# The second FFN of layer 0 in chunks of 4, 4, 4, 4 and 6, with its last down products begun from a doubled x in PSUM

## The chip, the core and the metric

The kernel is one program on one core of a Trainium2 chip. The core has five engines that run side by side, each with its own instruction queue: TensorE (PE in the profile; its weight loads are PEld), VectorE (DVE), ScalarE (ACT), GpSimd (POOL) and SyncE (SP). DMA queues bring data from memory into the on-chip buffer. TensorE writes its results into PSUM banks, from where VectorE and ScalarE read them. Engines wait for each other through semaphores. The metric is the device time of one execution, in microseconds; the median of three executions of the kernel before is 2505.7 us.

## The reference, cut to what matters

Two layers run over T = 640 tokens (512 of a prompt and 8 x 16 of running streams) of width D = 1024. Each has a half-step FFN, a mixer (a short convolution and banded attention, gated) and a second half-step FFN. All is fp32.

```
x = x + 0.5 * swiglu1(rmsnorm(x))
x = x + mixer(rmsnorm(x))
x = x + 0.5 * swiglu2(rmsnorm(x))

def swiglu(h):                       # FF = 2816
    g, u = split(h @ w_gu)           # 1024 x 5632
    return (silu(g) * u) @ w_down    # 2816 x 1024
```

The four FFNs are called a0, b0 (layer 0, before and after the mixer), a1 and b1 (layer 1). The change concerns b0, and the start of a1, which follows b0 directly.

## The kernel before

**Layout and products.** x is held transposed, as eight tiles `x[0]` to `x[7]` of 128 features by 640 tokens. An fp32 operand is split into a high part (a cast to the fp32r type) and a low part (what the cast left), and a product is made of three fp32r matmuls: high with high, low with high, high with low. Each covers 320 tokens, a half of the tokens (`HT`), and a 128 x 128 tile of weights. Weight slabs are fetched by DMA (`source`, L271), ScalarE casts their high part `whi` (L321) and VectorE subtracts for the low part `wlo` (L326).

**Seven products instead of eight.** The large products are made by a scheme that treats the operands as 2 x 2 blocks (the two halves of the tokens are one of the two block directions) and needs seven block products for eight, at the price of sums on VectorE. Their operands are called X11, X21, XN6, XT5, XT7, X22 and XT4. For x this is done in `Expand.final(m)` (L539): for each `x[m]` ScalarE squares it for the norm (L610), scales it (L559) and casts it, and VectorE makes sums and the low parts (L561 to L591). At odd m the sums need the even tile before, so the last cast (L576) waits for VectorE (L571). `Expand.weights(m)` (L594) takes care of the next slabs.

**An FFN.** The 22 feature tiles of FF are cut into chunks; `FFNS` (L46) lists the sizes of the chunks and how many tiles at the start go without the scheme. For each tile j, `gate_up` (L773) makes its gate and its up product in 84 matmuls (`paa`, `pba`, `pca` and so on in the profile), and a tail that ends in the activation, cast into `ahi` (L228) and its low part; the tail is put into the queues at a later place, and the last tile's after its last matmul. When a chunk is done, its down product is added to x during the next chunk. There are two ways:

- A chunk of exactly 4 tiles that isn't the last goes by seven (`by_seven`, L81). Two tiles make a `Pair` (L905), whose casts are ahead in `Pair.product`, and `down_rows` (L966) makes four outputs at a time, twice, behind gate-ups 1 and 2 of the next chunk: 84 matmuls each (L982), with results that ScalarE stages (L996, L999), GpSimd adds to x by accumulating DMAs (L1004), or VectorE takes straight from PSUM (L1009).
- Other chunks go plain: for each output m, `product` runs 6 matmuls per tile of the chunk (L388) into one PSUM accumulator, and VectorE does `x = 0.5 * pd + x` (L1119).

The last chunk is always plain, because nothing of this FFN follows to cover it: its eight products stand at the end, and as each `x[m]` comes out, `nxt.final(m)` prepares it for the next FFN. In b0 before, the chunks are 2, 4, 4, 4 and 8.

**Order and buffers.** The order of TensorE's, VectorE's and ScalarE's queues is that of the program text in most places. `flush` and `prep` in that text decide where a weight cast and its low part stand. From gate-up `free` (L1060) to the "cut" ahead of the last products only TensorE's order is fixed, and a scheduler sets the others. The accumulators of the plain products and of the rows come from a pool (`acc`) of two buffers of two banks each. The first gate-up of an FFN (`first` in `gate_up`) has an order of its own, in which the norm's sums of the new x are made as well.

Of the kernel before, what the change touches and what calls it, by code (L numbers as in the profile page):

```python
# [16 lines left out]
P = 128  # L17
# [25 lines left out]
NT = T // P  # L43


FFNS = {"a0": ((4, 4, 4, 4, 4, 2), 4), "b0": ((2, 4, 4, 4, 8), 0),  # L46
        "a1": ((4, 4, 4, 4, 4, 2), 0), "b1": ((3, 4, 4, 4, 4, 3), 0)}

PARTS = slice(0, 3 * P), slice(3 * P, T)
# [135 lines left out]
def halves(t):  # L185
    return t.rearrange("p (a b) -> p a b", a=2)
# [3 lines left out]
def trunk(ctx: ExitStack, tc: tile.TileContext, xin, wst, small, pbias, samplebias, kcache, vcache,  # L190
# [190 lines left out]
    def soon():  # L381
        return tc.high_priority(offset=300)

    def multiply(ps, ws, xs, first, last):
        (wh, wl), (xh, xl) = ws, xs
        for j, (w, x) in enumerate(((wh, xh), (wh, xl), (wl, xh))):
            for a in range(2):
                PE.matmul(ps[:, a, :HT], w, x[:, a * HT : (a + 1) * HT],  # L388
                          start=first and j == 0, stop=last and j == 2)

    def steps(ps, ops, at=()):


        n = len(ops)
        for k, (xh, xl) in enumerate(ops):
            if k in at:
                at[k]()
            multiply(ps, tiles.take(), (xh, xl), k == 0, k == n - 1)
            yield

    def product(ps, ops, at=()):
        for _ in steps(ps, ops, at):
            pass

    def block(ps, s, half, ops, ks, start, stop):
# [12 lines left out]
        ACT.dma_start(sm[:, c], small[:, c])  # L418
    ident = cp.tile([P, P], F32, name="ident")
    make_identity(nc, ident)  # L420
    ones = cp.tile([P, P], F32, name="ones")
    POOL.memset(ones, 1.0)
    fold = cp.tile([P, HP], F32, name="fold")
    POOL.tensor_tensor(out=fold, in0=ident[:, :HP], in1=ident[:, HP:], op=ALU.add)
# [48 lines left out]
    class Stats:  # L473
# [34 lines left out]
        @staticmethod  # L508
        def rows(ps, turned):

            for i in range(2):
                q = slice(i * HP, (i + 1) * HP)
                PE.matmul(ps[i], ones[q], turned[q, : ps[i].shape[1]], start=True, stop=True)

        def spread(self, ps, turned, out):

# [9 lines left out]
    class Expand(Stats):  # L526
# [67 lines left out]
        def weights(self, m):  # L594


            if m == KT - 3:
                source(used[0] + 3)
            elif m == KT - 1:
                self.flush()  # L600
                ahead()
                flush()
                begin()
# [126 lines left out]
    def seven(n, bank, X, c1, u2, c5, first, second, third, last):  # L730
# [39 lines left out]
        with soon():  # L770
            last(pa)

    def gate_up(fp, n, ex, first, tails, put, j, pair, later, at):  # L773

        pa, pb, pc = (att(f"p{i}{n}")[:, :HT] for i in "abc")

        def cap(name):
            return fp.tile([P, 2, HT], F32, tag="cap", name=f"{name}{n}", bufs=5)

        def mul(ps, s, half, x, ks, start, stop):  # L780
            block(ps, s, half, lambda kp: tuple(z[:, x] for z in ex.ops[kp]), ks, start, stop)

        def spot(name):
            step(later, f"g{at}{name}")

        every, most, end = range(NP), range(NP - 1), range(NP - 1, NP)
        g, u = tmp(f"g{n}"), tmp(f"u{n}")
        t1, t2 = slice(0, HT), slice(HT, T)
        both = cap("c1_")
        c1, u2, c5 = both[:, 0], both[:, 1], cap("c5_")[:, 0]  # L790
        rho = ex.rho
        if first:

            new = not ex.known
            s0, s1 = quiet(), quiet()
            mul(pa, s0, 0, X11, every, True, True)
            ACT.copy(c1, pa)
            if ex.rest:
                ex.rest()
            flush()  # L800
            if new:
                add(ex.ssum, ex.ssum, ex.sq6)
                ex.add()
            for t in tails[:2]:
                t()
            mul(pc, s1, 1, XT5, every, True, True)
            ACT.copy(c5, pc)
            if new:
                mul(pb, s0, 1, X21, most, True, True)
                mul(pa, s1, 0, XN6, most, False, True)  # L810
                mul(pb, s0, 1, X21, end, True, True)
                mul(pa, s1, 0, XN6, end, False, True)
            else:
                mul(pa, s1, 0, XN6, every, False, True)
                mul(pb, s0, 1, X21, every, True, True)
            ACT.copy(u2, pa)
            add(u[:, t1], pb, c1)
            for t in tails[2:]:
                t()
            tails.clear()  # L820
            s2 = quiet()
            prep(len(ready))
            flush()

            def third():
                mul(pc, s2, 1, X22, every, False, True)
                add(u[:, t2], pc, u2)

            if new:
                third()  # L830
                ex.total(acc(f"nps{n}")[:, 0])
                ex.root()
                ex.diagonal()
                prep(len(ready))
            mul(pa, s2, 0, XT7, every, False, True)
            add(g[:, t2], pa, c5)
            flush()
            if new:
                nbc = acc(f"nbc{n}")
                ex.spread([nbc[:, a, :HT] for a in range(2)])  # L840
            DVE.tensor_tensor(out=g[:, t2], in0=g[:, t2], in1=rho[:, t2], op=ALU.mult)
            if not new:
                third()
                prep(len(ready))
                flush()
            s3 = slab(True)[0]
        else:
            s0 = quiet()
            mul(pa, s0, 0, X11, every, True, True)
            ACT.copy(c1, pa)  # L850
            prep(used[0] + 1)
            spot("e1")
            for t in tails:
                t()
            tails.clear()
            spot("e2")
            flush()
            mul(pb, s0, 1, X21, every, True, True)
            add(u[:, t1], pb, c1)
            s1 = slab(True)[0]  # L860
            flush()
            mul(pa, s1, 0, XN6, every, False, True)
            ACT.copy(u2, pa)  # L863
            spot("e3")
            mul(pc, s1, 1, XT5, every, True, True)
            ACT.copy(c5, pc)
            s2 = slab(True)[0]
            spot("e4")
            mul(pa, s2, 0, XT7, every, False, True)
            add(g[:, t2], pa, c5)  # L870
            DVE.tensor_tensor(out=g[:, t2], in0=g[:, t2], in1=rho[:, t2], op=ALU.mult)
            flush()
            ahead()
            mul(pc, s2, 1, X22, every, False, True)
            add(u[:, t2], pc, u2)
            s3 = slab(True)[0]
            ahead()
        mul(pa, s3, 0, XT4, every, False, True)
        DVE.tensor_tensor(out=g[:, t1], in0=pa, in1=rho[:, t1], op=ALU.mult)
        ACT.activation(g, g, AF.Silu, scale=-1.0)  # L880
        spot("e7")
        flush()

        def tail(weights=True):
            if weights:
                begin()
            DVE.tensor_tensor(out=g, in0=g, in1=rho, op=ALU.mult)
            hi = hp.tile([P, T], F32R, tag="hhi", name=f"ahi{n}")
            lo = hp.tile([P, T], F32R, tag="hlo", name=f"alo{n}")
            if pair:  # L890
                pair.product(n, u, g, hi, lo)
            else:
                DVE.tensor_tensor(out=u, in0=u, in1=g, op=ALU.mult)
                flush()
                split(hi, lo, u)
            put(j, (hi, lo))
            if weights:
                ahead()

        tails.append(tail)  # L900

    class Pair:
# [5 lines left out]
            self.fp, self.name, self.i, self.later, self.spots = fp, name, i, later, spots  # L908
            self.E, self.X, self.done = None, {}, 0

        def product(self, n, u, g, hi, lo):
            if self.E is None:

                z = self.E = self.fp.tile([P, 3, HT], F32, name=f"de{n}", tag="even", bufs=1)
                DVE.tensor_tensor(out=z[:, 0:3:2], in0=halves(u), in1=halves(g), op=ALU.mult)
                DVE.tensor_tensor(out=z[:, 1], in0=z[:, 0], in1=z[:, 2], op=ALU.subtract)
                at, kinds = slice(0, 2), (X11, XT5)
            else:

                z = self.O = self.fp.tile([P, 5, HT], F32, name=f"do{n}", tag="odd", bufs=1)  # L920
                DVE.tensor_tensor(out=z[:, 3:5], in0=halves(u), in1=halves(g), op=ALU.mult)
                at, kinds = slice(3, 5), (X21, X22)
                self.later.append(self)
                self.work = self.rest()
            flush()
            ACT.copy(halves(hi), z[:, at])
            self.low(halves(lo), halves(hi), z[:, at])
            self.keep(kinds, hi, lo)

        def low(self, lo, hi, z):  # L930
            DVE.tensor_tensor(out=lo, in0=z, in1=hi.bitcast(F32), op=ALU.subtract)
# [117 lines left out]
    def ffn(name, fp, ex, goff, after, end=False):  # L1049
# [6 lines left out]
        last = FT - chunks[-1]  # L1056
        hold[0] = True

        mode = ExitStack()
        free = min(j for j in range(FT) if by_seven(name, j)) + 2  # L1060

# [7 lines left out]
        for what, a in ffn_order(name):  # L1069
# [29 lines left out]
            if end and js[0] == last:  # L1099
                nxt.all([act[j] for j in js])  # L1100
                break
            for m, js in a:
                if js[0] == last and m < 2 and first_two:

# [814 lines left out]
```

## Time and profile before

| | |
|---|---|
| runs | 2505.62, 2505.7 and 2506.22 us; median 2505.7 |
| profiled execution | 2506.73 us, of which the instruction span is 2505.0 us |
| mean granted TensorE clock | 0.998 of full speed |
| TensorE busy | 2487.9 us (99%), 17472 matmuls |
| VectorE busy | 2123.9 us (85%), 3443 instructions |
| ScalarE busy | 1322.0 us (53%), 2069 instructions |
| GpSimd busy | 254.2 us (10%), 378 instructions |

A row of the profile gives the start, the duration, the engine, the line of the program, the operation and its output and input tiles with shapes; `x12` says that twelve instructions alike are merged. Square brackets hold the idle time of that engine just ahead, and the engine, tile and line that ended it. The number and the letter behind a name (`pdb`, `paa`) are an FFN (a or b) and a part; numbers of tiles are left out. A row of grouped instructions has the count, then the busy time in us and the mean in ns, then the idle time ahead of them. A windows row gives for a stretch of the span the busy time of each engine with the number of its instructions, the granted clock, the share of the DMA engines and their GB/s. In this execution b0 runs from about 839 to 1257 us, and a1 follows it up to about 1670 us.

### The profile page before, as it was taken

The page shows a single profiled execution, that of the slowest core. Times are in us where ns is not written, and L with a number is a line of the kernel's source. Part 1 is how long each engine was busy: PE and PEld are TensorE (multiplying, and loading weights), DVE is VectorE, ACT ScalarE, POOL GpSimd, SP SyncE. Part 2 cuts the span into 40 slices and gives each one's busy share as a digit, 9 for nine tenths or more (in the row PEclk, how much of TensorE's full clock was granted, in tenths as well). Part 3 has the DMA queues.
Part 4 walks back from the last instruction along what each step waited for, and adds up shares of the span by engine and source line. Part 5 has one row for each costly group of instructions (what it writes and reads, how often), then busy time and mean ns, then how long its engine had stood idle before and what let it go on. Part 6 is the DMA issues. An engine that isn't in the chain of part 4 may idle for free.

```text
span 2505.0 us, 43861 instructions
## 1 busy us (share of the span) xinstructions
PE 2487.9 (99%) x17472; PEld 2433.1 (97%) x17472; DVE 2123.9 (85%) x3443; ACT 1322.0 (53%) x2069; POOL 254.2 (10%) x378
## 2 busy tenths in 40 slices
PE   9999999999999999999999999999999999999998
PEld 8999999889999999999999999998899999999998
DVE  7889998888677899998699999988786768899997
ACT  7445556664444545555455555556644455455553
POOL 0001112112000001110001111121210000011111
PEclk9999999999999999999999999999999999999999
DMA  4233445334222234443224343443432222244434
GB/s 145 76 102 103 121 116 127 108 122 156 77 87 92 76 102 116 108 108 101 85 75 110 110 121 103 116 118 118 140 136 85 77 93 78 86 113 109 121 101 103
DMA packets 101005, 265.47 MB, mean 106 GB/s; under 512 B 11360, under 2 KB 46816, under 8 KB 100800
## 3 DMA queue, kind: packets, MB, share of 16 engines
q1 hardware_dynamic: 69408, 220.76, 27.3%
q0 software_dynamic: 30528, 41.26, 9.3%
q8 instruction: 137, 2.24, 0.4%
q10 hardware_dynamic: 864, 0.65, 0.1%
q14 instruction: 68, 0.56, 0.1%
HBM read 222.70 MB, written 7.94 MB: 92 GB/s over the span
## 4 chain that ended last, share of the span: by engine, by line
PE 96%; DVE 2%; ACT 1%; DMA 1%; issue 0%; SPq 0%; DVEq 0%; ACTq 0%
PE pab L411 12%; PE paa L411 11%; PE pcb L411 6%; PE pca L411 6%; PE daa L982 5%; PE py L388 4%; PE po L388 4%; PE qa L411 4%; PE dab L982 4%; PE pdb L388 4%; PE pbb L411 3%; PE pba L411 3%; PE dca L982 3%; PE ma_cv L411 2%; PE ma_qk L411 2%; PE pda L388 2%
## 5 line engine op out<-in xcount | busy, mean ns | idle before, releaser
L321 ACT CAST whi<-raw 128x1024 fp32r<-128x1024 f32 (+1 forms) x566 | 509.5, 903 | 391.7 <-PE pbb L411 38.6
L326 DVE TENSOR_TENSOR wlo<-raw,whi 128x1024 fp32r<-128x1024 f32 (+1 forms) x566 | 585.4, 1037 | 137.7 <-ACT whi L321 135.5
L321 ACT CAST whi<-s 128x1024 fp32r<-128x1024 f32 (+1 forms) x152 | 144.4, 950 | 261.0 <-issue 89.5
L411 PE MATMUL pab<-xhib,whi 128*128 128x320 f32 x704 | 218.1, 310 | 0.0
L411 PE MATMUL pab<-xhib,wlo 128*128 128x320 f32 x704 | 217.3, 309 | 0.0
L411 PE MATMUL pab<-xlob,whi 128*128 128x320 f32 x704 | 217.3, 309 | 0.0
L411 PE MATMUL paa<-xhia,whi 128*128 128x320 f32 x640 | 198.1, 309 | 0.8 <-ACT c_a L863 0.5
L411 PE MATMUL paa<-xloa,whi 128*128 128x320 f32 x640 | 197.6, 309 | 0.0
L411 PE MATMUL paa<-xhia,wlo 128*128 128x320 f32 x640 | 197.6, 309 | 0.0
L326 DVE TENSOR_TENSOR wlo<-s,whi 128x1024 fp32r<-128x1024 f32 (+1 forms) x152 | 166.0, 1092 | 3.4 <-ACT whi L321 3.4
L1004 POOL DMA_DIRECT2D x<-c_b x56 | 49.2, 1017 | 1066.6 <-DVE x L1009 782.5
L1004 POOL DMA_DIRECT2D x<-c_a x72 | 63.4, 1017 | 831.6 <-ACT whi L321 508.0
L411 PEld LDWEIGHTS pab<-xhib,whi 128*128 128x128 f32 x704 | 132.1, 188 | 1.4 <-issue 0.9
L411 PEld LDWEIGHTS pab<-xlob,whi 128*128 128x128 f32 x704 | 132.1, 188 | 0.0
L411 PEld LDWEIGHTS pab<-xhib,wlo 128*128 128x128 f32 x704 | 132.1, 188 | 0.0
L411 PEld LDWEIGHTS paa<-xhia,whi 128*128 128x128 f32 x640 | 120.2, 188 | 1.8 <-ACT c_a L863 0.7
L411 PEld LDWEIGHTS paa<-xloa,whi 128*128 128x128 f32 x640 | 120.2, 188 | 0.0
L411 PEld LDWEIGHTS paa<-xhia,wlo 128*128 128x128 f32 x640 | 120.2, 188 | 0.0
L411 PE MATMUL pcb<-xhib,wlo 128*128 128x320 f32 x352 | 108.9, 309 | 0.0
L411 PE MATMUL pcb<-xhib,whi 128*128 128x320 f32 x352 | 108.7, 309 | 0.0
L411 PE MATMUL pcb<-xlob,whi 128*128 128x320 f32 x352 | 108.6, 309 | 0.0
L265 DVE TENSOR_TENSOR raw<-raw,raw 128x512 f32<-128x512 f32 x152 | 103.8, 683 | 1.8 <-DMA raw<-in_wst 1.3
(680 smaller groups left out, 7971.2 us busy)
## 6 DMA issues: line engine op xcount, KB each, us to landing
raw<-in_wst SPq DMA_DIRECT2D x378, 512.0 KB, 3.6
x<-c_a POOLq DMA_DIRECT2D x72, 160.0 KB, 4.2
x<-c_b POOLq DMA_DIRECT2D x56, 160.0 KB, 3.8
kc<-in_kcache SPq DMA_DIRECT2D x32, 256.0 KB, 3.7
vc<-in_vcache SPq DMA_DIRECT2D x16, 512.0 KB, 4.6
x<-u_a POOLq DMA_DIRECT2D x36, 160.0 KB, 4.2
x<-u_b POOLq DMA_DIRECT2D x28, 160.0 KB, 4.1
bias<-in_pbias POOLq DMA_DIRECT2D x16, 256.0 KB, 3.7
```

The costliest lines, as they stand in the source:

```text
L265: DVE.tensor_tensor(out=out, in0=a, in1=b, op=ALU.add)
L321: ACT.copy(hi[:, d], src[:, c])
L326: DVE.tensor_tensor(out=lo, in0=src, in1=hi.bitcast(F32), op=ALU.subtract)
L388: PE.matmul(ps[:, a, :HT], w, x[:, a * HT : (a + 1) * HT], start=first and j == 0, stop=last and j == 2)
L411: PE.matmul(ps, a, b, start=start and kp == 0 and j == 0, stop=stop and kp == NP - 1 and j == 2, skip_group_check=True)
L982: PE.matmul(ps[u], w, y, start=start and i == 0 and j == 0, stop=i == 1 and j == 2, skip_group_check=True)
L1004: POOL.dma_start(x[ms[2 * u + r]][:, cols], z[:, u], accum_op=ALU.add)
```

## The change

The chunks of b0 become 4, 4, 4, 4 and 6. One chunk more goes by seven, and the plain last chunk has 6 tiles instead of 8. Beside this:

- The eight last products of b0 no longer start from zero. ScalarE writes 2 x `x[m]` into the PSUM accumulator (`seed`), all matmuls accumulate onto it, and ScalarE, not VectorE, writes back `x[m]` as half of the result. Seeds 0 and 1 come ahead of product 0; seed m+1 stands in the program between the evacuation of `x[m-1]` with its `final`, and product m. Only b0 takes this way (`nxt` and a last chunk longer than 4).
- The first gate-up's pair casts its high part and subtracts its low part later: `held` keeps them until the `u2` copy of the next gate-up (a0's first pair, b0's and a1's).
- The column of ones for the norm's sums is one column wide and broadcast where it is used as a matrix.
- `weights` finds its next slab by a search instead of a fixed distance.

```
-FFNS = {"a0": ((4, 4, 4, 4, 4, 2), 4), "b0": ((2, 4, 4, 4, 8), 0),
+FFNS = {"a0": ((4, 4, 4, 4, 4, 2), 4), "b0": ((4, 4, 4, 4, 6), 0),
...
+    def seed(ps, m, scale):
+        ACT.activation(two(ps), halves(x[m]), AF.Copy, scale=scale)
...
-    def multiply(ps, ws, xs, first, last):
+    def multiply(ps, ws, xs, first, last, seeded=False):
...
-                          start=first and j == 0, stop=last and j == 2)
+                          start=first and j == 0 and not seeded, stop=last and j == 2,
+                          skip_group_check=seeded)
...
-    ones = cp.tile([P, P], F32, name="ones")
+    ones = cp.tile([P, 1], F32, name="ones")
...
-                PE.matmul(ps[i], ones[q], turned[q, : ps[i].shape[1]], start=True, stop=True)
+                PE.matmul(ps[i], ones[q].to_broadcast([HP, P]), turned[q, : ps[i].shape[1]], start=True, stop=True)
...
-                source(used[0] + 3)
+                source(next(i for i in range(used[0], len(slabs)) if slabs[i][0] == "gu" and slabs[i][2] == 1))
...
             ACT.copy(u2, pa)
+            for t in held:
+                t()
+            held.clear()
             spot("e3")
...
-                pair.product(n, u, g, hi, lo)
+                pair.product(n, u, g, hi, lo, held if first else None)
...
+            def parts():
+                ACT.copy(halves(hi), z[:, at])
+                self.low(halves(lo), halves(hi), z[:, at])
             self.keep(kinds, hi, lo)
+            if held is None:
+                parts()
+            else:
+                held.append(parts)
...
+        def seeded_down(name, a, js, nxt):
+            def begun(m):
+                pds[m] = acc(f"pd{name}_{js[0]}_{m}")
+                seed(pds[m], m, 2.0)
+            for m, _ in a:
+                if m == 0:
+                    begun(0)
+                if m + 1 < KT:
+                    begun(m + 1)
+                pd = pds.pop(m)
+                product(pd, [act[j] for j in js], seeded=True)
+                nxt.weights(m)
+                ACT.activation(halves(x[m]), two(pd), AF.Copy, scale=0.5)
+                if m < KT - 1:
+                    flush()
+                nxt.final(m)
...
+            if nxt and len(js) > 4:
+                seeded_down(name, a, js, nxt)
+                continue
```

More of the change, by code (lines that the diff above doesn't have):

```diff
@@ L388, in multiply, with steps @@
                 PE.matmul(ps[:, a, :HT], w, x[:, a * HT : (a + 1) * HT],
-                          start=first and j == 0, stop=last and j == 2)
-    def steps(ps, ops, at=()):
+                          start=first and j == 0 and not seeded, stop=last and j == 2,
+                          skip_group_check=seeded)
+    def steps(ps, ops, at=(), seeded=False):
         n = len(ops)
@@ L397, in steps, with product @@
                 at[k]()
-            multiply(ps, tiles.take(), (xh, xl), k == 0, k == n - 1)
+            multiply(ps, tiles.take(), (xh, xl), k == 0, k == n - 1, seeded)
             yield
-    def product(ps, ops, at=()):
-        for _ in steps(ps, ops, at):
+    def product(ps, ops, at=(), seeded=False):
+        for _ in steps(ps, ops, at, seeded):
             pass
@@ L771, in seven @@
             last(pa)
+    held = []
     def gate_up(fp, n, ex, first, tails, put, j, pair, later, at):
@@ L909, in __init__, with product @@
             self.E, self.X, self.done = None, {}, 0
-        def product(self, n, u, g, hi, lo):
+        def product(self, n, u, g, hi, lo, held=None):
             if self.E is None:
@@ L925, in product @@
             flush()
-            ACT.copy(halves(hi), z[:, at])
-            self.low(halves(lo), halves(hi), z[:, at])
+            def parts():
+                ACT.copy(halves(hi), z[:, at])
+                self.low(halves(lo), halves(hi), z[:, at])
             self.keep(kinds, hi, lo)
+            if held is None:
+                parts()
+            else:
+                held.append(parts)
         def low(self, lo, hi, z):
```

1 line of the change is left out of this document (added).

## The prediction, made before the changed kernel was run

> **What bounds the kernel now.** I read the page's busy shares first, then the chain that ended last, then that chain in order of time around the second FFN (b0).
>
> ```profile
> span 2505.0 us, 43861 instructions
> PE 2487.9 (99%) x17472; PEld 2433.1 (97%) x17472; DVE 2123.9 (85%) x3443; ACT 1322.0 (53%) x2069; POOL 254.2 (10%) x378
> PE 96%; DVE 2%; ACT 1%; DMA 1%; issue 0%; SPq 0%; DVEq 0%; ACTq 0%
> ```
>
> TensorE is busy for 99% of the span, and 96% of the chain is its own work. So removed matmuls pay one for one, and any gap opened in front of a matmul costs its full length. The chain, in order of time, at the change:
>
> ```profile
> 1198.79 1.76 PE pab L411 x12
> 1200.55 56.32 PE pdb L388 x384
> 1256.87 1.76 PE paa L411 x12
> ```
>
> The 384 matmuls of b0's last chunk (8 tiles x 6 matmuls x 8 outputs) take 56.32 us: 0.1467 us each, with nothing between them. Windows over all engines show what stands beside TensorE while chunks go by seven products, and in that last stretch:
>
> ```profile
> core 0: us, PE busy (x) PEld busy (x) DVE busy (x) ACT busy (x) POOL busy (x), PEclk, DMA share, GB/s
> 860.00:1130.00 270.00, 270.00 (x1842) 269.84 (x1841) 248.09 (x386) 137.42 (x199) 26.50 (x30) 1.00 0.41 109
> 1200.39:1256.71 56.32, 56.32 (x387) 56.32 (x386) 38.61 (x52) 27.58 (x35) 0.00 (x0) 1.00 0.20 66
> ```
>
> VectorE is at 248 of 270 us where chunks go by seven, near a bound but behind; in the last products it has a third of its time free. The change takes eight evacuations off it exactly there, where nothing waits for it.
>
> **The matmuls.** b0's plain products go from (2+8) x 8 x 6 = 480 matmuls to 6 x 8 x 6 = 288, its rows from 504 to 672 (a 4-chunk by seven costs 168 for 192). That is 24 fewer: 24 x 0.1467 = **-3.5 us**. The 20 takes, 12 accumulating POOL transfers and 12 stagings that the extra chunk adds run inside the by-seven regime above, where TensorE is 270.00 of 270.00: nothing, while VectorE stays under it. Two fewer weight transfers on SP and the narrower `ones` (the same two matmuls): nothing.
>
> **b0's opening.** Its first chunk now goes by seven from its first gate-up, as a1's already does. The same stretch of both, from 13.3 us into each FFN, TensorE alone, the first matmul of b0 (a1's is at the edge of the window above), and a1's waits:
>
> ```profile
> core 0: us, PE busy (x), PEclk, DMA share, GB/s
> 1270.00:1335.00 65.00, 63.85 (x430) 1.00 0.26 82
> 852.25:917.25 65.00, 65.00 (x444) 1.00 0.27 90
> 838.94 0.31 PE L411 MATMUL pab<-xhib,whi 128*128 128x320 f32 x1
> PE paa L411 <- ACT c_a L863: 0.5, 1, 0.5
> PE pca L411 <- ACT c_a L866: 0.4, 2, 0.2
> PE paa L411 <- ACT c_a L850: 0.3, 1, 0.3
> ```
>
> a1 does 14 matmuls fewer in 65 us: 14 x 0.1467 = 2.05 us, for 1.2 us of waits (each also costs a drain and a restart). All are ScalarE copies of `c1`, `u2` and `c5`, late behind the weight and operand casts. `held` moves the first pair's cast and subtraction behind the next gate-up's `u2` copy; that can shorten the L850 and L863 waits, 0.8 us of the 1.2, and leaves the two L866 ones. I take half of that 0.8 x 2.05/1.2 = 1.4 as saved: -0.7 (0 to -1.4) in a1, and b0's opening then costs 2.05 - 0.7 = +1.35 (0 to 2.05). Sum of both: **+0.7**. In a0 the same delay meets no wait: nothing.
>
> **The first seed.** In the order of the changed kernel as built, ScalarE's queue at b0's end is:
>
> ```
> ACT ... whi ; gb_21 (L890) ; ahib_21 <- ub_21 [waits VectorE] ; seed pdb_16_0 <- x_90 ; seed pdb_16_1 <- x_91 ; x_90 <- pdb_16_0 ; ...
> PE  ... pab_21 ; pdb_16_0 [waits ScalarE]
> ```
>
> TensorE has nothing else in its order between gate-up 21 and the first seeded product. Before, that product needed only tiles 14 to 20 for its first 42 matmuls, so tile 21's tail was hidden. That tail, in order of time on both engines, and two back-to-back ScalarE instructions of a later output:
>
> ```profile
> 1200.95 0.48 DVE L879 TENSOR_TENSOR gb<-pab,rhob 128x320 f32<-128x320 f32 x1
> 1201.47 0.74 ACT L880 ACTIVATE gb<-gb 128x640 f32<-128x640 f32 x1
> 1203.10 0.83 DVE L893 TENSOR_TENSOR ub<-ub,gb 128x640 f32<-128x640 f32 x1
> 1203.96 0.73 ACT L228 CAST ahib<-ub 128x640 fp32r<-128x640 f32 x1 [1.75 <-DVE ub L893]
> 1215.52 0.74 ACT L610 ACTIVATE sqa<-x 128x640 f32<-128x640 f32 x1 [3.34 <-DVE x L1119]
> 1216.17 0.82 ACT L559 ACTIVATE xoa<-x,sm 128x640 f32<-128x640 f32 x1
> ```
>
> The seed has its data long before, but it is queued behind `ahib`, which waits for all of this. The next ScalarE instruction of this size starts some 0.65 us after the one ahead of it (1216.17 after 1215.52): the seed starts near 1204.6. Its price isn't in the trace; the nearest rows are a PSUM-side copy (first) and an SBUF-side one (second) of the same 128x640:
>
> ```profile
> L996 ACT ACTIVATE c_b<-dab 128x640 f32<-128x640 f32 x6 | 4.2, 706 | 0.7
> L559 ACT ACTIVATE xoa<-x,sm 128x640 f32<-128x640 f32 x4 | 3.3, 818 | 0.0
> ```
>
> Between 0.71 and 0.82, I take 0.74, as the square at 1215.52: TensorE starts at 1205.4 instead of 1200.4 (the windows' edge): **+5.0** (4.7 to 5.4).
>
> **The clock.** What a pause does to the granted clock shows at the kernel's end and at its start:
>
> ```profile
> 2495.00:2497.00 2.00, 0.38 (x26) 0.22 (x16) 1.97 (x6) 0.68 (x2) 0.00 (x0) 1.00 0.56 193
> 2497.00:2499.00 2.00, 0.80 (x4) 0.50 (x4) 2.00 (x5) 0.00 (x0) 0.00 (x0) 0.50 0.63 222
> 5.12 0.90 PE L388 MATMUL poa<-hhia,whi 128*128 128x320 f32 x2 [5.12 <-ACT whi L650]
> 8.81 0.45 PE L388 MATMUL poa<-hhia,whi 128*128 128x320 f32 x2
> ```
>
> After 2 us with 0.38 busy the clock falls to 0.50. At the start the 12 matmuls between those last two rows take 3.69 us, against 12 x 0.1467 = 1.76: a cold restart costs 1.9. Five idle microseconds are longer than the 2 us that sufficed: **+1.9** (0 if the clock holds, 3.9 if it stays low twice as long). [...]
>
> **ScalarE's chain at odd outputs.** With two accumulators, seed m+1 must follow evacuation m-1 and be done before product m ends. At odd m the queue now holds evacuation, square, scale, cast, a cast that waits for VectorE, then the seed. The same chain before, from VectorE's evacuation on:
>
> ```profile
> 1214.66 0.82 DVE L1119 SCALAR_TENSOR_TENSOR x<-pdb,x 128x640 f32<-128x640 f32 x1 [4.19 <-PE pdb L388]
> 1218.20 0.49 DVE L571 TENSOR_TENSOR xoa<-xoa,xea 128x320 f32<-128x320 f32 x1
> 1218.72 1.00 ACT L576 CAST xhia<-xoa 128x960 fp32r<-128x960 f32 x1 [0.98 <-DVE xoa L571]
> 1219.63 1.04 ACT L321 CAST whi<-raw 128x1024 fp32r<-128x1024 f32 x1
> ```
>
> From 1214.66 to 1219.63 are 4.97; minus 0.11 (the evacuation at 0.71 for 0.82), plus the seed's 0.74 and 0.2 for the drain (a matmul's row is 0.31 long, its slot 0.147) and the signal: 5.8 us, against a product of 36 x 0.1467 = 5.28. It misses by 0.55 at m = 1 and 3 (at m = 5 six matmuls of a1's first gate-up stand ahead of product 7 in TensorE's built order, 0.88 us, and cover it): **+1.1** (0.4 to 1.8).
>
> **The hand-over to a1.**
>
> ```profile
> 1256.61 1.05 ACT L321 CAST whi<-raw 128x1024 fp32r<-128x1024 f32 x1 [2.19 <-PE pdb L388]
> 1256.91 0.82 DVE L1119 SCALAR_TENSOR_TENSOR x<-pdb,x 128x640 f32<-128x640 f32 x1
> 1257.77 0.74 ACT L610 ACTIVATE sqa<-x 128x640 f32<-128x640 f32 x1
> 1259.13 0.41 ACT L797 COPY c_a<-paa 128x320 f32<-128x320 f32 x1
> 1261.74 1.16 DVE L591 TENSOR_TENSOR xloa<-xoa,xhia 128x960 fp32r<-128x960 f32 x1 [0.33 <-ACT xhia L576]
> 1262.82 1.22 DVE L326 TENSOR_TENSOR wlo<-raw,whi 128x1024 fp32r<-128x1024 f32 x1
> ```
>
> ```
> PE  ... pdb_16_6 ; paa_0 x6 ; pdb_16_7 [waits ScalarE] ; paa_0 x6 ; ...
> ACT ... x_96 <- pdb_16_6 ; square, scale, cast of 6 ; c_a_0 <- paa_0 [waits PE] ; whi ; x_97 <- pdb_16_7 ; square, scale, casts of 7
> ```
>
> Before, x[7] is ready at 1257.73 and its operands at 1262.90, 5.17 later. In the built order above, ScalarE evacuates x[7] only behind the copy `c_a` (0.41), which waits for the other six of `paa`'s first twelve matmuls, after product 7 (0.88, and 0.2 of drain), and behind a `whi` cast (1.05): x[7] is ready about 3.2 us after product 7 ends, its operands at 3.2 + 5.17 - 0.4 (no `c_a` inside now) = 8.0. TensorE has 40 matmuls to fill until it needs them, 5.9. Short by 2.1; the next slab's `wlo`, queued behind them on VectorE, adds some 0.5: **+2.6** (1.0 to 3.8).
>
> **The sum.** -3.5 + 0.7 + 5.0 + 1.9 + 1.1 + 2.6 = +7.8. The profiled execution took 2506.7 us around its 2505.0 span, 1.0 above the runs' median of 2505.7; the change applied to the median gives **2513.5 us**. With every term at its low end (-3.5 - 1.4 + 4.7 + 0 + 0.4 + 1.0) it is +1.2, at its high end (-3.5 + 2.05 + 5.4 + 3.9 + 1.8 + 3.8) +13.5.
>
> **Rivals.** (A) The clock holds through the pause: -1.9, 2511.6. For it: inside the kernel no row of a low clock exists. Against: the end's row.
>
> (B) ScalarE becomes the bound of all eight products, or the hand-over's gap slows the clock a second time. ScalarE is at 27.58 of 56.32 us before, and eight seeds and eight evacuations of 0.74 add 11.8: at most 39 us of a shorter 42.2. At 93% in order, with its waits, it could miss at every output, 8 x 0.3 more than I count; a second restart is 1.9. About +2.2: 2515.7.
>
> (C) Other side: the first seed doesn't hold TensorE, because its write is done before 1200.4. Then pause and restart go, -6.9: +0.9, 2506.6; with the odd chain and the hand-over at their low ends (-2.3), 2504.3. It decides by whether the seed ends before gate-up 21's last matmul; the built queue, `ahib` ahead of it, speaks against.
>
> (D) The seven-product chunk doesn't pay in b0 since VectorE (92% there) is pushed over TensorE in the opening: up to 3 us beyond a1's 2.05, 2516.5. a1, which opens the same way, speaks against.
>
> **How the numbers follow.** Forecast 0.55, A 0.18, B 0.13, C 0.08, D 0.06. Range 2507.5 to 2518.0: low from A with a short hand-over (2511.6 - 1.6 - 0.7 - 1.4 = 2507.9) and just above C, high beyond B and D. What this measurement can tell from no change is 0.2%, 5.0 us: slower is above 2510.7. Of C a third is faster by that much at most: 0.03. Of the forecast a tenth, of A four in ten, and the rest of C lie within it: 0.06 + 0.07 + 0.05 = 0.18. Slower 0.79.
>
> **What would show it.** 17448 matmul records. TensorE idle for some 5 us before b0's first seeded product, released by ScalarE, and a clock below 1 just behind it; if that idle is under 1 us, the seed step is wrong. Waits of 0.4 to 0.6 us before the third and fifth seeded products on ScalarE's seed; if these appear at every output, B. Some 2 to 3 us of idle at a1's start on `xhi`, `xlo` or `wlo`; the L863 wait shorter in a1. L866 waits of 0.2 new in b0's opening. The prediction is wrong if ScalarE passes `ahib`, or if a low clock lasts over 8 us.

## The result, and the profile after

The changed kernel takes 2515.8 us (median of 5 runs, 2515.0 to 2516.5) against 2506.2 us (5 runs, 2505.6 to 2506.8): 1.0039 times as long, 95% interval 1.0028 to 1.0050. It is slower by 9.6 us; 7.8 were forecast, and the time lies inside the range of 2507.5 to 2518.0.

The page of the changed kernel, in the rows that answer to those shown of before:

```profile
span 2513.0 us, 43899 instructions
PE 2489.3 (99%) x17448; PEld 2433.2 (97%) x17448; DVE 2132.5 (85%) x3465; ACT 1341.0 (53%) x2099; POOL 264.1 (11%) x390
PE 94%; DVE 3%; ACT 1%; issue 1%; DMA 0%; DVEq 0%; ACTq 0%; POOLq 0%
```

The 24 matmuls are gone (17448 for 17472). TensorE's share of the chain fell from 96% to 94%; two per cent of the span are 50 us, so these shares can't show a loss of 9.6 us. TensorE's waits show it (by engine, line, and what was waited for: us in total, times, the longest), first in b0's opening, from 838 to 925 us, then from the last gate-up of b0 to a1's opening, 1190 to 1350 us:

```profile
PE pab L416 <- DVE wlo L326: 0.5, 2, 0.3
PE pcb L416 <- ACT c_b L876: 0.4, 2, 0.2
...
PE pdb L392 <- ACT pdb L386: 4.8, 1, 4.8
PE pba L416 <- DVE xloa L596: 1.0, 1, 1.0
PE paa L416 <- DVE xloa L596: 0.8, 1, 0.8
PE paa L416 <- DVE wlo L326: 0.6, 2, 0.3
PE pca L416 <- ACT c_a L876: 0.4, 2, 0.2
PE pca L416 <- DVE wlo L326: 0.3, 1, 0.3
```

Line numbers are each kernel's own; in the changed one L386 is the seed, L392 the former L388, L416 the former L411, L876 the former L866, L596 the former L591. The longest wait is the one before the first seeded product. In order of time, ScalarE, and then TensorE's first seeded rows:

```profile
1213.00 0.74 ACT L890 ACTIVATE gb<-gb 128x640 f32<-128x640 f32 x1
1215.48 0.72 ACT L228 CAST ahib<-ub 128x640 fp32r<-128x640 f32 x1 [1.75 <-DVE ub L903]
1216.11 1.32 ACT L386 ACTIVATE pdb<-x 128x640 f32<-128x640 f32 x2
1216.87 0.56 PE L392 MATMUL pdb<-ahib,whi 128*128 128x320 f32 x2 [4.79 <-ACT pdb L386]
```

The two seeds stand directly behind `ahib`, as in the built order; the first takes 1.32 / 2 = 0.66 us and lets TensorE go. The granted clock in stretches around that place (PEclk is the number behind GpSimd's busy time), and at a1's start. The two rows at 0.50 begin and end where the clock changed, 3.41 us apart; the others stand beside them and are about as long:

```profile
1213.89:1217.30 3.41, 0.43 (x3) 0.43 (x4) 3.38 (x4) 1.82 (x3) 0.00 (x0) 1.00 0.38 132
1217.31:1220.71 3.40, 3.40 (x15) 3.40 (x15) 0.01 (x1) 0.13 (x1) 0.00 (x0) 0.50 0.42 154
1220.72:1224.10 3.38, 3.38 (x25) 3.38 (x25) 0.00 (x0) 0.06 (x1) 0.00 (x0) 1.00 0.00 0
1268.51:1271.91 3.40, 1.59 (x8) 1.10 (x8) 3.08 (x4) 1.88 (x4) 0.00 (x0) 1.00 0.00 0
1271.92:1275.32 3.40, 3.40 (x46) 3.07 (x50) 2.84 (x5) 1.65 (x2) 0.00 (x0) 0.50 0.49 154
```

The clock is low twice, for 3.41 us each time: behind the pause, and once more behind the waits of a1's start. What leads to those waits, three rows of ScalarE and one of VectorE:

```profile
1263.55 0.42 ACT L804 COPY c_a<-paa 128x320 f32<-128x320 f32 x1 [2.16 <-PE paa L416]
1263.87 1.05 ACT L321 CAST whi<-raw 128x1024 fp32r<-128x1024 f32 x1
1264.83 0.70 ACT L1092 ACTIVATE x<-pdb 128x640 f32<-128x640 f32 x1
1269.53 1.16 DVE L596 TENSOR_TENSOR xloa<-xoa,xhia 128x960 fp32r<-128x960 f32 x1 [0.32 <-ACT xhia L581]
```

The last matmul of product 7 starts at 1262.33 and takes its slot of 0.147 us. Behind it ScalarE still has the copy `c_a` and a weight cast, and writes x[7] by 1265.53, 3.1 us later. The last operand made from it is there at 1270.69.

To set kernels side by side, a stretch is used that holds all that the change touches here: from b0's first matmul to the last late `c5` copy in a1's opening. In the kernel before it runs from the row at 838.94, shown in the prediction, to this row:

```profile
1330.97 0.41 PE L411 MATMUL pca<-xhia,whi 128*128 128x320 f32 x1 [0.18 <-ACT c_a L866]
```

In the changed kernel it runs from the first of these two rows to the second:

```profile
838.10 0.31 PE L416 MATMUL pab<-xhib,whi 128*128 128x320 f32 x1
1339.98 0.42 PE L416 MATMUL pca<-xhia,whi 128*128 128x320 f32 x1 [0.18 <-ACT c_a L876]
```

That is 492.03 and 501.88 us: +9.85, so all of the loss is in it. The spans alone differ by 8.0 only. Of the 1.85 us between, 0.84 lie ahead of b0's first matmul: the profiled execution of the kernel before has a wait of 0.7 us in the mixer that the changed kernel's hasn't (other kernels' executions have it too). The other 1.0 lie behind the stretch, in many small pieces that the change doesn't touch. Counted as what TensorE's starts lie apart beyond 0.1467 us each, the +9.85 is made of:

| part | us |
|---|---|
| 24 matmuls fewer | -3.5 |
| b0's opening | +1.7 |
| pause before the first seeded product | +5.0 |
| 12 matmuls at half clock behind it, 0.267 us each | +1.4 |
| two waits for a seed, 0.36 each, and small gaps | +1.0 |
| hand-over to a1 (three waits) | +3.2 |
| 9 matmuls at half clock behind it | +1.1 |
| a1's opening, with the delayed cast | -0.2 |

Their sum is +9.7; the rest is in gaps too small to count.

### The profile page after: what moved, and what is told of

Same layout as the page of the kernel before. It is cut to its first block, busy times and chain, and to the rows that moved or that the text cites. A ratio compares the mean times of both kernels' runs of the same rounds, so it can differ in the third digit from the quotient of the medians.

```text
span 2513.0 us, 43899 instructions
## 1 busy us (share of the span) xinstructions
PE 2489.3 (99%) x17448; PEld 2433.2 (97%) x17448; DVE 2132.5 (85%) x3465; ACT 1341.0 (53%) x2099; POOL 264.1 (11%) x390
## 4 chain that ended last, share of the span: by engine, by line
PE 94%; DVE 3%; ACT 1%; issue 1%; DMA 0%; DVEq 0%; ACTq 0%; POOLq 0%
PE pab L416 12%; PE paa L416 11%; PE pcb L416 6%; PE pca L416 5%; PE daa L999 5%; PE dab L999 4%; PE py L392 4%; PE po L392 4%; PE qa L416 4%; PE pbb L416 3%; PE pba L416 3%; PE dca L999 3%; PE poa L392 2%; PE pdb L392 2%; PE ma_cv L416 2%; PE ma_qk L416 2%
## 5 line engine op out<-in xcount | busy, mean ns | idle before, releaser
L416 PE MATMUL pab<-xhib,wlo 128*128 128x320 f32 x704 | 217.5, 309 | 0.5 <-DVE wlo L326 0.5
L416 PE MATMUL pab<-xhib,whi 128*128 128x320 f32 x704 | 217.8, 309 | 0.0
L416 PE MATMUL pab<-xlob,whi 128*128 128x320 f32 x704 | 217.3, 309 | 0.0
L416 PE MATMUL paa<-xloa,whi 128*128 128x320 f32 x640 | 197.6, 309 | 0.8 <-DVE xloa L596 0.8
L416 PE MATMUL paa<-xhia,wlo 128*128 128x320 f32 x640 | 197.7, 309 | 0.6 <-DVE wlo L326 0.6
L416 PE MATMUL paa<-xhia,whi 128*128 128x320 f32 x640 | 197.7, 309 | 0.0
L1021 POOL DMA_DIRECT2D x<-c_b x64 | 56.2, 1019 | 1091.3 <-DVE x L1026 751.0
L416 PEld LDWEIGHTS pab<-xhib,whi 128*128 128x128 f32 x704 | 132.2, 188 | 1.1 <-issue 0.9
L416 PEld LDWEIGHTS pab<-xhib,wlo 128*128 128x128 f32 x704 | 132.1, 188 | 1.1 <-DVE wlo L326 1.1
L416 PEld LDWEIGHTS pab<-xlob,whi 128*128 128x128 f32 x704 | 132.2, 188 | 0.0
L416 PEld LDWEIGHTS paa<-xhia,wlo 128*128 128x128 f32 x640 | 120.1, 188 | 1.1 <-DVE wlo L326 1.1
L416 PEld LDWEIGHTS paa<-xloa,whi 128*128 128x128 f32 x640 | 120.1, 188 | 1.0 <-DVE xloa L596 1.0
L416 PEld LDWEIGHTS paa<-xhia,whi 128*128 128x128 f32 x640 | 120.1, 188 | 0.5 <-issue 0.4
L416 PE MATMUL pcb<-xhib,whi 128*128 128x320 f32 x352 | 108.9, 309 | 0.4 <-ACT c_b L876 0.4
L416 PE MATMUL pcb<-xhib,wlo 128*128 128x320 f32 x352 | 108.9, 309 | 0.0
L416 PE MATMUL pcb<-xlob,whi 128*128 128x320 f32 x352 | 108.7, 309 | 0.0
```

Of the source, the lines that this page charges most:

```text
L416: PE.matmul(ps, a, b, start=start and kp == 0 and j == 0, stop=stop and kp == NP - 1 and j == 2, skip_group_check=True)
L1021: POOL.dma_start(x[ms[2 * u + r]][:, cols], z[:, u], accum_op=ALU.add)
```

## The experiments

All kernels of this table were timed against the kernel before on the same chip (2506.2 us beside the changed kernel, 2505.5 to 2505.6 beside the others). "Stretch" is the difference of the stretch above to the kernel before, in one profiled execution.

| kernel | median us | ratio, 95% interval | stretch us |
|---|---|---|---|
| changed kernel | 2515.8 | 1.0039 (1.0028 to 1.0050) | +9.85 |
| first two seeds early | 2509.5 | 1.0015 (1.0006 to 1.0024) | +2.73 |
| TensorE filled in the pause | 2513.1 | 1.0032 (1.0020 to 1.0045) | +8.00 |
| seeds, old chunks | 2513.0 | 1.0029 (1.0018 to 1.0039) | +7.12 |
| new chunks, no seeds | 2505.9 | 1.0001 (0.9992 to 1.0010) | +0.36 |
| delayed cast alone | 2505.3 | 0.9997 (0.9988 to 1.0006) | -0.22 |
| no seeds, first two products side by side | 2507.3 | 1.0005 (0.9996 to 1.0013) | +0.55 |
| seeds early and beside the evacuations | 2508.8 | 1.0010 (1.0001 to 1.0019) | +2.11 |
| all repairs, first two side by side | 2510.6 | 1.0018 (1.0009 to 1.0027) | +6.90 |
| seeds beside, mended hand-over | 2508.0 | 1.0008 (0.9999 to 1.0017) | +1.43 |
| the same, one tile ahead | 2507.8 | 1.0006 (0.9997 to 1.0015) | +1.89 |
| no seeds, one tile ahead | 2505.2 | 0.9997 (0.9989 to 1.0006) | -0.45 |

For four kernels (first two seeds early, no seeds with two side by side, seeds beside, mended hand-over) the median lies 1.0 to 1.3 us further above the kernel before than the stretch does. Their profiled executions have a mean clock of 0.999; of the ten others of each, four to eight have 0.998 or less. A fall of the clock at a1's start in those, worth 1.1 us in the table above, would account for it. That is not shown, since those executions were not profiled; the small steps below are therefore checked against the stretch.

**Is it the queue ahead of the first seed?** The first two seeds are put into the program ahead of the last tile's tail; in ScalarE's queue they then stand in the rows behind gate-up 18 (1169.1 us) and in gate-up 19 (1178.1 us).

```
+            if js[0] == last and after is not None and len(js) > 4 and a[0][0] == 0:
+                begun(js, 0)
+                begun(js, 1)
             if js[0] == last or len(a) * len(js) >= KT:
                 for t in tails:
                     t()
...
             for m, _ in a:
-                if m == 0:
-                    begun(0)
-                if m + 1 < KT:
-                    begun(m + 1)
+                if 0 < m < KT - 1:
+                    begun(js, m + 1)
```

> Seeds 0 and 1 stand in ScalarE's queue during gate-ups 18 and 19, so that no tail is ahead of them; all else as in the changed kernel. My theory (the first seed, behind the last tile's cast, holds TensorE, and the pause slows the clock): the 4.95 us gap before the first seeded product goes, and the 12 slow matmuls behind it (1.44 us) too: 2515.8 - 6.4 = 2509.4 us. Rival (the pause is made by something else at this place, the weights of the first product or the PSUM banks): the gap stays above 3 us, 2513 us or more.

It took 2509.5 us, 3.9 above the kernel before where the changed one is 9.6 above. TensorE's waits, 1190 to 1350 us:

```profile
PE pba L416 <- DVE xloa L596: 1.0, 1, 1.0
PE paa L416 <- DVE xloa L596: 0.8, 1, 0.8
PE paa L416 <- DVE wlo L326: 0.6, 2, 0.3
PE pdb L392 <- DVE alob L229: 0.5, 1, 0.5
...
```

The wait of 4.8 for the seed is gone: the queue was the cause. A new wait of 0.5 (0.8 with its drain and restart) has come in its place, for `alob`, the low part of the last tile's activation; the pause had covered it.

**Is it the pause that slows the matmuls behind it?**

```
                 if m == 0:
+                    idle = att("idle")[:, :HT]
+                    hi = ex.ops[0][0]
+                    for i in range(33):
+                        PE.matmul(idle, hi[:, 0, :P], hi[:, 1], start=True, stop=True)
                     begun(0)
```

> The changed kernel with 33 matmuls whose result nobody reads (33 x 0.147 = 4.84 us) between gate-up 21 and the first seeded product, where TensorE is idle: TensorE does not pause, and the seed comes no earlier. My theory (the slow matmuls behind the pause are the clock's answer to the pause): they run at 0.147 us each, 2515.8 - 1.4 = 2514.4 us. Rival (they are slow because ScalarE writes seed 1 and VectorE subtracts a weight's low part beside them, or for another reason of this place): the 12 matmuls still take 0.267 each, 2515.8 us.

It took 2513.1 us, 7.5 above the kernel before, 2.1 less than the changed kernel, with 33 matmuls more. The windows around the same place:

```profile
1211.00:1216.00 5.00, 5.00 (x36) 5.00 (x35) 4.16 (x6) 2.88 (x4) 0.00 (x0) 1.00 0.31 110
1216.00:1220.00 4.00, 4.00 (x28) 3.78 (x27) 0.73 (x1) 0.85 (x2) 0.00 (x0) 1.00 0.34 131
```

TensorE is busy throughout (5.00 of 5.00 and 4.00 of 4.00 us) and the clock stays at 1.00 while the same seeds are written. So the slow matmuls came with the pause and its low clock, 1.4 us; the wait for the seed is unchanged. The rest of the 2.1 is within what single medians differ by.

**Do the seeds cost without the new chunks?** `FFNS` as before and no delayed cast, but the seeded last products.

```
-FFNS = {... "b0": ((4, 4, 4, 4, 6), 0),
+FFNS = {... "b0": ((2, 4, 4, 4, 8), 0),
```

> The chunks of before (2, 4, 4, 4, 8) and no delayed cast, but the last eight products seeded. My theory: the first gap of 4.95 and the slow matmuls of 1.44 come as in the changed kernel; the odd gaps don't, since a product of 48 matmuls is 7.0 us long against a chain of 5.8; at the hand-over no matmuls of a1 are moved ahead of product 7, so 0.5 to 1.5 us: 2506.2 + 7.4 = 2513.6 us (2512.8 to 2514.5). Rival (the seeds cost only with the short products of 6 tiles): under 2510 us.

2513.0 us, 7.4 above the kernel before, as expected: the pause of 4.95 (a wait of 4.8 for the seed) is there, no wait for a later seed, and 0.5 us at the hand-over. That leaves 1.7 of the stretch's 7.12, room for the 1.4 of slow matmuls behind the pause, though no row of the clock shows them in this run. With products of 7.0 us the pause and what follows it are nearly the whole loss.

**Do the chunks pay without the seeds?** The branch to `seeded_down` is taken out.

```
-            if nxt and len(js) > 4:
-                seeded_down(name, a, js, nxt)
-                continue
```

> The chunks, the delayed cast of the first pair, the narrow ones and the search of the changed kernel, but the last products as before: from zero, with VectorE's evacuation. My theory (24 matmuls saved, b0's opening 1.8 us worse, a1's 0.2 better, and the whole loss in the seeds): 2506.2 - 3.5 + 1.8 - 0.2 = 2504.3 us, with no gap at the start of the last products and under 0.5 us at a1's start. Rival (the chunks cost time themselves, since VectorE or the opening loses more than the matmuls give): 2506.5 us or more.

A miss: 2505.9 us, 0.4 above the kernel before on its chip, where 1.9 below was expected; no difference can be told, and the stretch is 0.36 us longer. TensorE's waits, 1190 to 1350 us:

```profile
PE paa L416 <- DVE xloa L596: 0.8, 1, 0.8
PE paa L416 <- DVE wlo L326: 0.6, 2, 0.3
PE pdb L392 <- DVE alob L229: 0.6, 1, 0.6
PE pca L416 <- ACT c_a L876: 0.4, 2, 0.2
PE pca L416 <- DVE wlo L326: 0.3, 1, 0.3
```

VectorE and ScalarE at the last tile's tail, in order of time:

```profile
1216.68 1.22 DVE L326 TENSOR_TENSOR wlo<-raw,whi 128x1024 fp32r<-128x1024 f32 x1
1216.79 0.73 ACT L228 CAST ahib<-ub 128x640 fp32r<-128x640 f32 x1 [1.75 <-DVE ub L903]
1217.81 0.82 DVE L229 TENSOR_TENSOR alob<-ub,ahib 128x640 fp32r<-128x640 f32 x1
```

Two covers had gone with the two tiles. With 8 tiles the last tile's activation was needed after 42 matmuls (6.2 us); with 6 it is needed after 30 (4.4 us), and `alob` comes 1.0 us later than that (1218.63 us), 0.8 us lost. And at the hand-over TensorE loses 1.4 us more: VectorE evacuates x[7] late. The evacuations of x[6] and x[7] and TensorE's first matmul of a1:

```profile
1251.99 0.82 DVE L1157 SCALAR_TENSOR_TENSOR x<-pdb,x 128x640 f32<-128x640 f32 x1
1256.34 0.31 PE L416 MATMUL paa<-xhia,whi 128*128 128x320 f32 x1
1257.16 0.68 DVE L265 TENSOR_TENSOR raw<-s,raw 128x512 f32<-128x512 f32 x1
1257.76 0.81 DVE L1157 SCALAR_TENSOR_TENSOR x<-pdb,x 128x640 f32<-128x640 f32 x1
```

In the kernel before VectorE evacuated x[7] at 1256.91, 0.2 us after its product; here at 1257.76, 1.4 us after it (1256.34), with no idle time ahead. From one of these evacuations to the other VectorE took 5.77 us; the product is 5.28. In the kernel before all eight evacuations come 0.2 us after their product; here the last three are 0.8, 0.9 and 1.4 us behind. So -3.5 + 1.7 (b0's opening) + 0.8 (`alob`) + 1.4 (hand-over) - 0.2 = +0.2, and the stretch says +0.36.

**The delayed cast alone.** `held` and `parts` put into the kernel before, nothing else.

> The kernel before with nothing but the delayed cast and subtraction of the first pair. My theory: only a1's opening has waits that it can touch; they shrink by 0.2 us (1.30 to 1.09 with drains, as between the runs with and without it): 0.2 us below the kernel before, too little to be told from no change. Rival of the prediction: 0.7 us or more are saved there.

2505.3 us, no difference to the kernel before; the stretch is 0.22 us shorter, and in a1's opening the two waits of TensorE for the copies at L850 and L863 (0.8 together) have become two waits for `wlo` (0.6). By the stretch the size of my theory holds and the prediction's 0.7 doesn't; the medians alone can't tell 0.2 from 0.7.

**Is the tail's missing cover to be had back?** First with the two-products order that the kernel has for last chunks of 4 tiles:

```
-        first_two = FFNS[name][0][-1] == 4
+        first_two = FFNS[name][0][-1] in (4, 6)
```

> The unseeded kernel (chunks 4, 4, 4, 4, 6), in which the first two of the last products run side by side, so that tile 21 is needed after 60 matmuls (8.8 us) instead of 30 (4.4 us). My theory: a last chunk of 6 covers the last tile's tail no longer; the 0.7 us gap at alo goes: 0.7 below the unseeded kernel. Rival: x[0] comes out 5 us later, VectorE falls behind by as much, and a1's opening gives the 0.7 us back.

The rival was right: in the stretch +0.55 for +0.36 without it (the medians, 2507.3 and 2505.9, lie further apart, see below the table). The `alob` wait went (TensorE's gaps in the eight products fell from 0.9 to 0.3 us), but x[0] came out 3.6 us later, and a1's start lost 0.7 us more, in a new wait for `xloa` at `pba`. Then with only one tile of product 1 ahead of tile 21 of product 0:

```
+    for j, w in zip(js[:-1], w0):
+        multiply(pds[0], w, act[j], j == js[0], False)
+    multiply(pds[1], tiles.take(), act[js[0]], True, False, False)
+    multiply(pds[0], w0[-1], act[js[-1]], False, True)
```

> The unseeded kernel, with the same six matmuls of product 1 ahead of tile 21 of product 0. My theory: 0.7 below the unseeded kernel, so 0.3 to 0.5 below the kernel before, too little to be told from no change; a1's opening still loses 4.4 us against 3.2, since VectorE needs some 5.8 us (evacuation 0.8, two low parts of 1.2, one of 0.8, a sum of 0.5, two weight sums of 0.7) for an odd output's rest and an even output, against a product of 5.3. Rival: as for the kernel before this one.

2505.2 us; the stretch is -0.45, 0.8 less than without it, and a1's start is unchanged: the wait for `alob` is gone and nothing was given back. Against the kernel before it is 0.9997 times (0.9989 to 1.0006): the best version with the new chunks, and not to be told from the kernel before.

**Are the waits for a later seed order or load?** Seed m+2 directly behind the evacuation of `x[m]`, on top of the early first seeds:

```
-                if 0 < m < KT - 1:
-                    begun(js, m + 1)
                 pd = pds.pop(m)
                 product(pd, [act[j] for j in js], seeded=True)
                 nxt.weights(m)
                 ACT.activation(halves(x[m]), two(pd), AF.Copy, scale=0.5)
+                if m + 2 < KT:
+                    begun(js, m + 2)
```

> The kernel with the early first seeds, in which seed m+2 stands directly behind the evacuation of x[m], ahead of its square, scale and casts. My theory (the two waits at odd outputs are ScalarE's order, not its load): both 0.36 us gaps go, 0.7 below the kernel with early seeds; a1's opening as there. Rival (ScalarE is the bound of these products): the gaps stay or come later, no change.

2508.8 us, 0.7 below the kernel with early seeds (0.6 in the stretch), and both gaps are gone: it was the order. In the changed kernel the chain was (ScalarE, m = 3):

```profile
1240.18 0.71 ACT L1092 ACTIVATE x<-pdb 128x640 f32<-128x640 f32 x1 [0.68 <-PE pdb L392]
1240.93 0.74 ACT L615 ACTIVATE sqa<-x 128x640 f32<-128x640 f32 x1
1241.57 0.82 ACT L564 ACTIVATE xoa<-x,sm 128x640 f32<-128x640 f32 x1
1242.42 0.73 ACT L572 CAST xhia<-xoa 128x640 fp32r<-128x640 f32 x1
1243.87 1.00 ACT L581 CAST xhia<-xoa 128x960 fp32r<-128x960 f32 x1 [0.73 <-DVE xoa L576]
1244.78 0.70 ACT L386 ACTIVATE pdb<-x 128x640 f32<-128x640 f32 x1
```

From 1240.18 to the seed's end at 1245.48 are 5.3 us.

**Is the hand-over order or load?** All repairs together first, with the first two products side by side, product 7 unseeded, and the copy `c1` of a1's first gate-up on VectorE; then the last two of these without the side-by-side order.

```
-            ACT.copy(c1, pa)
+            if n == "a1_0":
+                DVE.tensor_copy(c1, pa)
+            else:
+                ACT.copy(c1, pa)
...
+                if m < KT - 1:
                     ACT.activation(halves(x[m]), two(pd), AF.Copy, scale=0.5)
+                else:
+                    DVE.scalar_tensor_tensor(out=halves(x[m]), in0=two(pd), scalar=0.5,
+                                             in1=halves(x[m]), op0=ALU.mult, op1=ALU.add)
```

> All of it together: seeds 0 and 1 early, the first two products side by side, each seed beside the evacuation, product 7 from zero with VectorE's evacuation, and the copy c1 of a1's first gate-up on VectorE instead of ScalarE, so that ScalarE's square of x[7] follows at once. My theory: only the matmuls saved (-3.5), b0's opening (+1.8), the delayed cast (-0.2) and 0 to 0.6 of hand-over are left: 1.3 to 1.9 us below the kernel before. Rival (the loss at a1's start comes from VectorE's and ScalarE's load in the shorter products, whatever the order): 1 us above it or more.

> The kernel with the seeds early and beside the evacuations, in which product 7 starts from zero with VectorE's evacuation, and VectorE makes the copy c1 of a1's first gate-up: ScalarE's square of x[7] then has neither the copy nor its own evacuation ahead of it, and no matmuls of a1 are moved ahead of product 7. My theory (the loss at the hand-over is the order around x[7], since the seven seeded evacuations take VectorE's load away): of the 6.2 us that TensorE loses in the first 100 us of a1, against 3.2 before, some 2.2 go; 2.2 below the kernel with the seeds beside. Rival (VectorE is behind by its load): no more than 0.5 below.

> As the kernel with the mended hand-over, and the six matmuls of tile 16 of product 1 run ahead of tile 21 of product 0, so that alo of tile 21 is needed 0.88 us later and x[0] comes no later. My theory: the 0.7 us gap at alo goes, nothing is given back, 0.7 below that kernel and about the time of the kernel before. Rival: given back in a1's opening, as when the first two products ran side by side.

The first was a clear miss: 2510.6 us. Both accumulators fill at once, so product 2 waits 1.5 us for its seed, x[0] comes 4.2 us later than with the seeds beside, and the mean clock of its profiled execution is 0.997, for 0.999 with the seeds beside. The second is 0.7 us below the kernel with the seeds beside, where 2.2 were expected and the rival said at most 0.5: between the two. So the order around x[7] was part of it; what the rest is, order or load, isn't shown. Its ScalarE rows show where x[6] is late, product 6 having ended at 1249.55 (the start of product 7's first matmul):

```profile
1249.55 0.46 PE L392 MATMUL pdb<-ahib,whi 128*128 128x320 f32 x2
1249.77 1.00 ACT L581 CAST xhia<-xoa 128x960 fp32r<-128x960 f32 x1 [1.79 <-DVE xoa L576]
1250.67 1.04 ACT L321 CAST whi<-s 128x1024 fp32r<-128x1024 f32 x1
1251.62 0.70 ACT L1092 ACTIVATE x<-pdb 128x640 f32<-128x640 f32 x1
```

x[6] is evacuated 2.1 us after its product, because the casts of x[5], which had waited 1.79 us for VectorE, are ahead of it in ScalarE's queue. That is not ScalarE's load alone, since it stood idle for those 1.79 us; VectorE, too, is busy for 16.5 of the 19.7 us up to 1263.2, and waits for ScalarE in the rest. With the evacuations on VectorE, VectorE is late (with x[7] by 1.4 us in the kernel with no seeds); with them on ScalarE, ScalarE is (here with x[6] by 2.1). The third lost the `alob` gap, but its stretch is 0.46 us longer, in a profiled execution with a mean clock of 0.998, for 0.999 in that of the one before it; a fall of the clock at a1's start (1.1 us in the changed kernel) would account for it, which is not shown. Its median of 2507.8 is 0.2 below the one before it.

## Why the prediction was right, step by step

- **The matmuls**, -3.5: right, 24 fewer. That VectorE's lighter last stretch is worth nothing, since "nothing waits for it" there, was wrong: with 6-tile products VectorE's evacuation of x[7] is late by 1.2 us in the kernel with no seeds.
- **b0's opening**, +1.35, and **a1's**, -0.7, together +0.7: measured +1.7 and -0.2, +1.5. The waits came where a1 has them; the step that failed is that the delayed cast saves half. It replaces waits for copies by waits for `wlo`, and saves 0.2.
- **The first seed**, +5.0: measured 4.95, and shown by the run with early seeds and by the seeds with the old chunks.
- **The clock**, +1.9: that the pause brings the slow matmuls is shown by the filled pause; 12 matmuls at 0.267 instead of 0.147 us are 1.4. The clock was at 0.50 for 3.41 us behind a pause of 4.8. The 1.9 was too much: it was taken from 12 matmuls at the kernel's start, 3.69 us, of which 12 at 0.267 are 3.2. The other 0.5 us look like waits, by an estimate from the starts of the pairs: they lie up to 0.70 us apart, where two at 0.267 take 0.53. That the clock was low there was the author's estimate too; the view of 5.00 to 9.00 us shows 1.00.
- **ScalarE's chain at odd outputs**, +1.1: 0.7, behind the two chains named, of outputs 1 and 3. The waits stand before products 3 and 5 counted from 0, the fourth and the sixth, where the prediction's list of signs says third and fifth. Each was 0.36 for 0.55, in part since VectorE, without the evacuations, made its sums 0.25 us sooner (0.73 us of idle time ahead of the cast in the row at 1243.87, for 0.98 in the kernel before).
- **The hand-over**, +2.6: 3.2, in waits for `xloa` and `wlo` as named, 0.6 more than taken and inside its bounds. The path is the one predicted: x[7] is ready 3.1 us after product 7 (3.2 said), and its last operand at 1270.69, 8.2 us after it (8.0 said). A second fall of the clock, which stood in rival B only, cost 1.1 more. Part of the cause was not seen: in the run with no seeds at all the hand-over still loses 1.4.
- **What it missed.** The shorter last chunk itself takes two covers away, 0.8 us at `alob` and the 1.4 at the hand-over, so that the chunks are worth +0.2 to +0.4 instead of the -2.8 that the first two steps add up to. In the changed kernel the pause hid the first of these and the hand-over step held the second, so the sum came out near. That it is only 1.9 us off is partly luck: the clock and the odd outputs were taken 0.9 us too high together, which pays back some of the openings (0.8 too low), the hand-over (0.6) and the second fall (1.1).

Of the rivals, A (no fall of the clock) fell, and so did C (the seed holds TensorE indeed). B's second restart came, its eight missed outputs did not. D is not borne out: b0's opening costs 1.7 us, no more than a1's.

## What to carry to other kernels

An operation that must run before a matmul starts (a seed in PSUM, where a plain start needs none) came here only as early as its place in ScalarE's queue: behind the last tile's cast it held TensorE for 4.8 us, ahead of the tail not at all. Look at what that queue is waiting for at this moment, and put the operation ahead of it. Before a last stage is shortened to save matmuls, list what it hides: here each product covered 5.3 us of the next stage's preparation instead of 7.0, and the last tile's tail was needed 1.8 us sooner, which ate 2.2 of the 3.5 us saved; the opening by seven took most of the rest. A pause on TensorE can cost more than its length: here 4.95 us, and 1.4 us of slow matmuls behind it.

## What was not expected of the hardware

The same waits at a1's start were followed by a low clock in the changed kernel and not with early seeds. In the changed kernel (two waits of 1.0 and 0.8 us, above) the clock was at 0.50 for 3.41 us from 1271.92 on, behind 3.40 us in which TensorE was busy for 1.59. The ten matmuls behind these waits in the changed kernel (first row), then with early seeds, where the same two waits of 1.0 and 0.8 come before them, and a stretch of that run that holds the wait of 0.8 and nearly all of these matmuls:

```profile
1271.88 3.03 PE pca L416 x10
1268.16 1.73 PE pca L416 x10
1266.00:1269.60 3.60, 2.56 (x16) 2.05 (x15) 3.57 (x4) 2.06 (x4) 0.00 (x0) 1.00 0.11 19
```

With early seeds the clock stayed at 1.00 in this stretch, and the ten matmuls took 1.73 us instead of 3.03. These are two executions, one of each kernel; why the clock fell in one of them isn't shown, and it was not tried to move the waits.
